# Moving one channel sum of the last image group from VectorE to ScalarE in a color-constancy kernel

## Chip, cores, metric

One core of a Trainium2 chip. The metric is device time in microseconds of one execution, median over runs. The sets of rounds ran on different chips, and the kernel before had a median of 22.99 to 23.03 us in each.

## The reference

```python
def reference(image):                      # float32 [16, 128, 128, 3]
    mean_rgb = np.mean(image, axis=(1, 2), keepdims=True)
    gray = np.mean(mean_rgb, axis=-1, keepdims=True)
    scale = gray / (mean_rgb + 1e-10)
    return np.clip(image * scale, 0, 1).astype(np.float32)
```

Every image has to be read wholly (three channel sums) before its first pixel can be scaled. The data is 3.15 MB in and 3.15 MB out, and it stays in SBUF, the core's own memory, in between. PSUM, named below, is the memory into which TensorE writes its results.

## The kernel before

Sixteen images are handled in four groups of four (g0 to g3). A group is one tile of 128 partitions x 512 pixels x 3 channels, 32 partitions per image.

```python
for g in range(G):                                     # G = 4
    nc.sync.dma_start(out=img_g, in_=src)              # L: load, 768 KB
    for c in range(2):                                 # A: ScalarE, sums of channels 0 and 1
        nc.scalar.activation(out=scr_p[:, 0:Q], in_=img_g[:, :, c], func=act.Copy,
                             accum_out=rows_g[:, c : c + 1])
    nc.vector.reduce_sum(out=rows_g[:, 2:3], in_=img_g[:, :, 2], axis=ax.X)   # R: VectorE, channel 2
    nc.tensor.matmul(psum_g, lhsT=blk, rhs=rows_g, start=True, stop=True)     # M: totals per image
    # D: denominator and total (from PSUM), C: reciprocal, S: scale   -- three tiny VectorE steps
    ... cut ...
    if g == G - 1:
        chunks = [(0, 320, nc.sync), (320, Q, nc.scalar)]   # last group: two stores
    else:
        chunks = [(0, Q, nc.sync)]
    for q0, q1, eng in chunks:
        for c in range(C):                             # O: VectorE, multiply and clip
            nc.vector.tensor_scalar(out=out_g[:, q0:q1, c], in0=img_g[:, q0:q1, c],
                scalar1=scale_g[:, c : c + 1], scalar2=1.0, op0=alu.mult, op1=alu.min)
        eng.dma_start(out=dst[:, q0 * C : q1 * C], in_=out_g[:, q0:q1, :])
```

The letters are used below: D3 is step D of group g3. The order on each engine is chosen by a scheduler. On VectorE it is R0 R1 D0 C0 S0 O0, D1 **R2** C1 S1 O1, D2 **R3** C2 S2 O2, D3 C3 S3 O3.

## Time and profile before

| | before |
|---|---|
| time, median of 16 runs in the rounds with the changed kernel | 23.0 us (22.92 to 23.1) |
| span of the profiled execution | 21.2 us |
| busy: VectorE / ScalarE / TensorE | 11.5 / 8.8 / 2.3 us |
| R: 4 reductions, mean | 825 ns |
| A: 8 ACTIVATEs, mean (plus accumulator read) | 853 ns (189 ns) |
| O: multiply pass over 512 pixels, mean | 560 ns |

Read it in stages: the loads keep DMA full to about 9.6 us (their last packets end at 10.5), then the stores follow as VectorE finishes each group, with pauses between them, and the last of them fill 4 us without a pause. VectorE is 54% busy over the span, but from 6.96 to 17.50 us it hardly rests (10.19 of 10.54 us busy). The lines are in the prediction.

### The profile page before, as it was taken

To read this page: it belongs to the slowest core of one execution; us is meant where nothing else is said; L and a number is where in the kernel's file an instruction comes from. 1 tells how busy PE (TensorE), PEld (TensorE's weight loads), DVE (VectorE), ACT (ScalarE), POOL (GpSimd) and SP (SyncE) were. 2 spreads that over 40 slices of the span, in tenths; PEclk is the share of its full clock that TensorE was granted. 3 is DMA by queue.
4 is the path that set the end of the run, shared out by engine and by line. 5 is a ranking of instruction groups with operands and counts; after the bars stand their busy time and mean duration, and the time that the engine had idled before them with its cause. 6 is when DMAs were issued, how large, how long until landed. Compare 5 with 4: busy or idle time off the path is not lost.

```text
span 21.2 us, 133 instructions
## 1 busy us (share of the span) xinstructions
PE 2.3 (11%) x8; PEld 2.0 (9%) x8; DVE 11.5 (54%) x40; ACT 8.8 (42%) x17; POOL 0.2 (1%) x4
## 2 busy tenths in 40 slices
PE   0000000000000550090046000540000000000000
PEld 0000000000000540090045000630000000000000
DVE  0360000003920898999989999899989990000000
ACT  0698000003999999999999991000000000000000
POOL 3000000000000000000000000000000000000000
DMA  0006999999999999983089980889708998999500
GB/s 0 0 0 151 325 395 406 418 418 395 418 395 430 406 430 441 406 360 128 23 360 383 395 348 0 372 372 453 290 0 372 430 430 335 436 399 376 196 0 0
DMA packets 1296, 6.29 MB, mean 297 GB/s; under 512 B 144, under 2 KB 144, under 8 KB 1296
## 3 DMA queue, kind: packets, MB, share of 16 engines
q1 hardware_dynamic: 1152, 6.00, 70.2%
q10 hardware_dynamic: 144, 0.29, 3.6%
HBM read 3.15 MB, written 3.15 MB: 297 GB/s over the span
## 4 chain that ended last, share of the span: by engine, by line
DVE 47%; DMA 27%; issue 2%; SPq 2%; DVEq 2%
DVE out_g L105 29%; DMA img_g<-in_image_dram 27%; DVE rows_g L69 11%; DVE scale_g L90 3%; DVE recip_g L88 3%; SPq L61 2%; DVE denom_g L78 2%; DVEq L139 2%
## 5 line engine op out<-in xcount | busy, mean ns | idle before, releaser
L63 ACT ACTIVATE scr_p<-img_g 128x512 f32<-128x512 f32 x8 | 6.8, 853 | 3.2 <-DMA img_g<-in_image_dram 3.1
L105 DVE TENSOR_SCALAR out_g<-img_g,scale_g 128x512 f32<-128x512 f32 (+2 forms) x15 | 6.4, 493 | 0.1
L69 DVE TENSOR_REDUCE rows_g<-img_g 128x1 f32<-128x512 f32 x4 | 3.3, 825 | 4.6 <-DMA img_g<-in_image_dram 4.6
L74 PE MATMUL psum_g<-rows_g,blk 128*128 128x3 f32 x8 | 2.3, 361 | 11.7 <-ACT scr_p L63 9.7
L74 PEld LDWEIGHTS psum_g<-rows_g,blk 128*128 128x128 f32 x8 | 2.0, 312 | 11.9 <-ACT scr_p L63 11.9
L63 ACT ACT_TABLE_LOAD x1 | 1.3, 1283 | 0.7 <-PEq L128 0.7
L63 ACT ACTIVATION_READ_ACCUMULATOR scr_p<-img_g 128x1 f32 x8 | 1.5, 189 | 0.0
L90 DVE SCALAR_TENSOR_TENSOR scale_g<-recip_g,tot_g 128x3 f32<-128x3 f32 x4 | 0.6, 161 | 0.1
L88 DVE RECIPROCAL recip_g<-denom_g 128x3 f32<-128x3 f32 x4 | 0.7, 167 | 0.1
L78 DVE TENSOR_SCALAR_CACHE_REDUCE denom_g<-psum_g 128x3 f32<-128x3 f32 x4 | 0.6, 156 | 0.0
L46 DVE MEMSET blk<- 128x128 f32 x1 | 0.2, 165 | 0.8 <-PEq L128 0.8
L48 DVE MEMSET blk<- 32x32 f32 x4 | 0.3, 85 | 0.2
L78 DVE DVE_READ_ACCUMULATOR denom_g<-psum_g 128x1 f32 x4 | 0.3, 84 | 0.0
L128 POOL MEMSET const-bfloat16-1.0<- 128x1 bf16 x1 | 0.1, 103 | 0.0
L128 POOL MEMSET const-float32-0.0<- 128x1 f32 x1 | 0.1, 100 | 0.2 <-issue 0.2
L128 POOL MEMSET const-uint8-127<- 128x1 uint8 x1 | 0.1, 102 | 0.0
L128 POOL MEMSET const-float32-1.0<- 128x1 f32 x1 | 0.1, 99 | 0.0
## 6 DMA issues: line engine op xcount, KB each, us to landing
img_g<-in_image_dram SPq DMA_DIRECT2D x4, 768.0 KB, 6.5
out_dram<-out_g SPq DMA_DIRECT2D x3, 768.0 KB, 3.3
out_dram<-out_g SPq DMA_DIRECT2D x1, 480.0 KB, 2.9
out_dram<-out_g ACTq DMA_DIRECT2D x1, 288.0 KB, 2.8
```

The source lines that it names most:

```text
L46: nc.vector.memset(blk, 0.0)
L48: nc.vector.memset(blk[j * PPB : (j + 1) * PPB, j * PPB : (j + 1) * PPB], 1.0)
L61: nc.sync.dma_start(out=img_g, in_=src)
L63: nc.scalar.activation(out=scr_p[:, 0:Q], in_=img_g[:, :, c], func=act.Copy, accum_out=rows_g[:, c : c + 1],)
L69: nc.vector.reduce_sum(out=rows_g[:, 2:3], in_=img_g[:, :, 2], axis=ax.X,)
L74: nc.tensor.matmul(psum_g, lhsT=blk, rhs=rows_g, start=True, stop=True)
L78: nc.vector.tensor_scalar(out=denom_g, in0=psum_g, scalar1=float(eps_sum), scalar2=None, op0=alu.add, op1=alu.add, accum_out=tot_g,)
L88: nc.vector.reciprocal(recip_g, denom_g)
L90: nc.vector.scalar_tensor_tensor(out=scale_g, in0=recip_g, scalar=1.0 / 3.0, in1=tot_g.broadcast_to([P, C]), op0=alu.mult, op1=alu.mult,)
L105: nc.vector.tensor_scalar(out=out_g[:, q0:q1, c], in0=img_g[:, q0:q1, c], scalar1=scale_g[:, c : c + 1], scalar2=1.0, op0=alu.mult, op1=al ...
L128: nc = _bacc.Bacc("TRN2", target_bir_lowering=False, num_devices=1)
L139: with _tile.TileContext(nc) as tc:
```

## The change

The intent is to shorten VectorE's work after the loads: the third sum of g3 goes to ScalarE, which is idle by then. The loop is also rewritten as a list of stages, traced in the order given, so that the scheduler no longer chooses.

```diff
+    ON_ACT = (3,)  # groups whose third sum ScalarE does too
+    PROGRAM = "L0 L1 L2 L3 A0 R0 M0 A1 R1 M1 D0 C0 S0 O0 D1 A2 R2 M2 C1 S1 O1 D2 A3 M3 C2 S2 O2 D3 C3 S3 O3".split()
...
-        for c in range(2):
-            nc.scalar.activation(
+            for c in range(3 if g in ON_ACT else 2):
+                pin(nc.scalar.activation(
                     out=scr_p[:, 0:Q], in_=..., func=act.Copy, accum_out=...[:, c : c + 1])
-        nc.vector.reduce_sum(out=rows_g[:, 2:3], in_=img_g[:, :, 2], axis=ax.X)
+        elif what == "R":  # VectorE: sum of channel 2
+            pin(nc.vector.reduce_sum(out=t["rows"][:, 2:3], in_=t["img"][:, :, 2], axis=ax.X))
...
+    for word in PROGRAM:
+        stage(word[0], int(word[1:]))
```

The list has no R3, and A3 has three sums. `pin` keeps an instruction in its place on its engine. Everything else builds to the same instructions in the same order, but for one added wait (O3's first pass also waits for load 3).

More of the change, by code (lines that the diff above doesn't have):

```diff
@@ L20 @@
     assert C == 3
-    G = 4
-    BPG = B // G
-    assert BPG * G == B
-    PPB = P // BPG
-    ROWS_PER_PART = (H * BPG) // P
-    Q = ROWS_PER_PART * W
+    sizes = [4, 4, 4, 4]
+    assert sum(sizes) == B
+    G = len(sizes)
     f32 = mybir.dt.float32
@@ L39 @@
     const = ctx.enter_context(tc.tile_pool(name="const", bufs=1))
-    io = ctx.enter_context(tc.tile_pool(name="io", bufs=G))
-    st = ctx.enter_context(tc.tile_pool(name="st", bufs=G))
-    ps = ctx.enter_context(tc.tile_pool(name="ps", bufs=G, space=bass.MemoryType.PSUM))
+    io = ctx.enter_context(tc.tile_pool(name="io", bufs=4))
+    st = ctx.enter_context(tc.tile_pool(name="st", bufs=4))
+    ps = ctx.enter_context(tc.tile_pool(name="ps", bufs=4, space=bass.MemoryType.PSUM))
     psd = ctx.enter_context(tc.tile_pool(name="psd", bufs=2, space=bass.MemoryType.PSUM))
-    blk = const.tile([P, P], f32, name="blk")
@@ L46 @@
-    nc.vector.memset(blk, 0.0)
-    for j in range(BPG):
-        nc.vector.memset(blk[j * PPB : (j + 1) * PPB, j * PPB : (j + 1) * PPB], 1.0)
-    for g in range(G):
-        rows = slice(g * (P * ROWS_PER_PART), (g + 1) * (P * ROWS_PER_PART))
-        src = img_rows[rows].rearrange("(p k) x -> p (k x)", k=ROWS_PER_PART)
-        dst = out_rows[rows].rearrange("(p k) x -> p (k x)", k=ROWS_PER_PART)
-        img_g = io.tile([P, Q, C], f32, name="img_g")
-        out_g = io.tile([P, Q, C], f32, name="out_g")
-        rows_g = st.tile([P, C], f32, name="rows_g")
-        psum_g = ps.tile([P, C], f32, name="psum_g")
-        scr_p = psd.tile([P, Q], f32, name="scr_p")
-        nc.sync.dma_start(out=img_g, in_=src)
-        for c in range(2):
-            nc.scalar.activation(
-                out=scr_p[:, 0:Q],
-                in_=img_g[:, :, c],
-                func=act.Copy,
-                accum_out=rows_g[:, c : c + 1],
-            )
-        nc.vector.reduce_sum(
-            out=rows_g[:, 2:3],
-            in_=img_g[:, :, 2],
-            axis=ax.X,
-        )
-        nc.tensor.matmul(psum_g, lhsT=blk, rhs=rows_g, start=True, stop=True)
-        denom_g = st.tile([P, C], f32, name="denom_g")
-        tot_g = st.tile([P, 1], f32, name="tot_g")
-        nc.vector.tensor_scalar(
-            out=denom_g,
-            in0=psum_g,
-            scalar1=float(eps_sum),
-            scalar2=None,
-            op0=alu.add,
-            op1=alu.add,
-            accum_out=tot_g,
-        )
-        recip_g = st.tile([P, C], f32, name="recip_g")
-        nc.vector.reciprocal(recip_g, denom_g)
-        scale_g = st.tile([P, C], f32, name="scale_g")
-        nc.vector.scalar_tensor_tensor(
-            out=scale_g,
-            in0=recip_g,
-            scalar=1.0 / 3.0,
-            in1=tot_g.broadcast_to([P, C]),
-            op0=alu.mult,
-            op1=alu.mult,
-        )
-        if g == G - 1:
-            chunks = [(0, 320, nc.sync), (320, Q, nc.scalar)]
-        else:
-            chunks = [(0, Q, nc.sync)]
-        for q0, q1, eng in chunks:
-            for c in range(C):
-                nc.vector.tensor_scalar(
-                    out=out_g[:, q0:q1, c],
-                    in0=img_g[:, q0:q1, c],
-                    scalar1=scale_g[:, c : c + 1],
-                    scalar2=1.0,
-                    op0=alu.mult,
-                    op1=alu.min,
-                )
-            eng.dma_start(out=dst[:, q0 * C : q1 * C], in_=out_g[:, q0:q1, :])
@@ new lines @@
+    blks = {}
+    for gb in sorted(set(sizes)):
+        ppb = P // gb
+        t = const.tile([P, P], f32, name=f"blk{gb}")
+        nc.vector.memset(t, 0.0)
+        for j in range(gb):
+            nc.vector.memset(t[j * ppb : (j + 1) * ppb, j * ppb : (j + 1) * ppb], 1.0)
+        blks[gb] = t
+    ON_ACT = (3,)
+    PROGRAM = "L0 L1 L2 L3 A0 R0 M0 A1 R1 M1 D0 C0 S0 O0 D1 A2 R2 M2 C1 S1 O1 D2 A3 M3 C2 S2 O2 D3 C3 S3 O3".split()
+    row0 = [sum(sizes[:g]) for g in range(G)]
+    S = [dict() for _ in range(G)]
@@ new lines, in stage @@
+    def stage(what, g):
+        t, GB = S[g], sizes[g]
+        rpp = (H * GB) // P
+        Q = rpp * W
+        rows = slice(row0[g] * H, (row0[g] + GB) * H)
+        pin = tc.keep_in_program_order
+        if what == "L":
+            src = img_rows[rows].rearrange("(p k) x -> p (k x)", k=rpp)
+            t["img"] = io.tile([P, Q, C], f32, name="img_g", tag=f"img{Q}")
+            pin(nc.sync.dma_start(out=t["img"], in_=src))
+        elif what == "A":
+            t["rows"] = st.tile([P, C], f32, name="rows_g")
+            scr_p = psd.tile([P, Q], f32, name="scr_p", tag=f"scr{Q}")
+            for c in range(3 if g in ON_ACT else 2):
+                pin(nc.scalar.activation(
+                    out=scr_p[:, 0:Q],
+                    in_=t["img"][:, :, c],
+                    func=act.Copy,
+                    accum_out=t["rows"][:, c : c + 1],
+                ))
+        elif what == "R":
+            pin(nc.vector.reduce_sum(
+                out=t["rows"][:, 2:3], in_=t["img"][:, :, 2], axis=ax.X
+            ))
+        elif what == "M":
+            t["psum"] = ps.tile([P, C], f32, name="psum_g")
+            nc.tensor.matmul(t["psum"], lhsT=blks[GB], rhs=t["rows"], start=True, stop=True)
+        elif what == "D":
+            t["denom"] = st.tile([P, C], f32, name="denom_g")
+            t["tot"] = st.tile([P, 1], f32, name="tot_g")
+            pin(nc.vector.tensor_scalar(
+                out=t["denom"],
+                in0=t["psum"],
+                scalar1=float(eps_sum),
+                scalar2=None,
+                op0=alu.add,
+                op1=alu.add,
+                accum_out=t["tot"],
+            ))
+        elif what == "C":
+            t["recip"] = st.tile([P, C], f32, name="recip_g")
+            pin(nc.vector.reciprocal(t["recip"], t["denom"]))
+        elif what == "S":
+            t["scale"] = st.tile([P, C], f32, name="scale_g")
+            pin(nc.vector.scalar_tensor_tensor(
+                out=t["scale"],
+                in0=t["recip"],
+                scalar=1.0 / 3.0,
+                in1=t["tot"].broadcast_to([P, C]),
+                op0=alu.mult,
+                op1=alu.mult,
+            ))
+        elif what == "O":
+            dst = out_rows[rows].rearrange("(p k) x -> p (k x)", k=rpp)
+            out_g = io.tile([P, Q, C], f32, name="out_g", tag=f"out{Q}")
+            if g == G - 1:
+                chunks = [(0, (Q * 5) // 8, nc.sync), ((Q * 5) // 8, Q, nc.scalar)]
+            else:
+                chunks = [(0, Q, nc.sync)]
+            for q0, q1, eng in chunks:
+                for c in range(C):
+                    pin(nc.vector.tensor_scalar(
+                        out=out_g[:, q0:q1, c],
+                        in0=t["img"][:, q0:q1, c],
+                        scalar1=t["scale"][:, c : c + 1],
+                        scalar2=1.0,
+                        op0=alu.mult,
+                        op1=alu.min,
+                    ))
+                pin(eng.dma_start(out=dst[:, q0 * C : q1 * C], in_=out_g[:, q0:q1, :]))
```

## The prediction

> **What bounds the kernel now.** The four image groups are called g0 to g3. For each: load (L), sums of channels 0 and 1 on ScalarE (A), sum of channel 2 on VectorE (R), a matmul that spreads totals (M), then on VectorE denominator (D), reciprocal (C), scale (S) and three multiply-and-clip passes (O), then a store. I read the page first (VectorE is busy 54% of the span, no engine is full on average), then the chain of work that ended last, in order of time, because a mean over load, middle and tail says nothing about the end:
>
> ```profile
> 6.96 0.83 DVE rows_g L69
> ...
> 12.49 0.07 DVE denom_g L78 x2
> 12.57 0.74 DVE rows_g L69
> 13.30 0.09 DVE recip_g L88
> 13.40 0.02 issue
> 13.42 0.17 DVE scale_g L90
> ```
>
> From 6.96 us, when g1's load lands, the chain stays on VectorE to 17.50 us. At 12.57 it holds a reduction that has nothing to do with g2, whose scale is being computed: it is R3, the sum for the next group, which the scheduler put between D2 and C2. The timeline, VectorE alone, shows the same with starts and lengths (first column start, second length, us):
>
> ```profile
> 12.40 0.16 DVE L78 TENSOR_SCALAR_CACHE_REDUCE denom_g<-psum_g 128x3 f32<-128x3 f32 x1
> 12.48 0.09 DVE L78 DVE_READ_ACCUMULATOR denom_g<-psum_g 128x1 f32 x1
> 12.48 0.82 DVE L69 TENSOR_REDUCE rows_g<-img_g 128x1 f32<-128x512 f32 x1
> 13.22 0.17 DVE L88 RECIPROCAL recip_g<-denom_g 128x3 f32<-128x3 f32 x1
> 13.42 0.16 DVE L90 SCALAR_TENSOR_TENSOR scale_g<-recip_g,tot_g 128x3 f32<-128x3 f32 x1
> 13.62 1.49 DVE L105 TENSOR_SCALAR out_g<-img_g,scale_g 128x512 f32<-128x512 f32 x3
> 15.02 0.15 DVE L78 TENSOR_SCALAR_CACHE_REDUCE denom_g<-psum_g 128x3 f32<-128x3 f32 x1
> 15.10 0.08 DVE L78 DVE_READ_ACCUMULATOR denom_g<-psum_g 128x1 f32 x1
> 15.21 0.17 DVE L88 RECIPROCAL recip_g<-denom_g 128x3 f32<-128x3 f32 x1
> ```
>
> Here D2 to C2 (12.40 to 13.22) takes 0.82 us; D3 to C3 (15.02 to 15.21), with no reduction between, takes 0.19. ScalarE and TensorE for g3, in the same timeline:
>
> ```profile
> 10.80 0.87 ACT L63 ACTIVATE scr_p<-img_g 128x512 f32<-128x512 f32 x1
> 11.58 0.19 ACT L63 ACTIVATION_READ_ACCUMULATOR scr_p<-img_g 128x1 f32 x1
> 11.80 0.86 ACT L63 ACTIVATE scr_p<-img_g 128x512 f32<-128x512 f32 x1
> 12.60 0.19 ACT L63 ACTIVATION_READ_ACCUMULATOR scr_p<-img_g 128x1 f32 x1
> 13.42 0.50 PEld L74 LDWEIGHTS psum_g<-rows_g,blk 128*128 128x128 f32 x2 [2.04 <-ACT scr_p L63]
> 13.45 0.56 PE L74 MATMUL psum_g<-rows_g,blk 128*128 128x3 f32 x2 [1.98 <-DVE recip_g L88]
> ```
>
> ScalarE is done at 12.79 and stays idle until it issues the last store. M3 waited for R3, not for ScalarE. The last view is the busy time in stretches; columns are stretch, length, busy us of PE, PEld, DVE, ACT, POOL, then clock, DMA share, GB/s:
>
> ```profile
> 12.60:13.30 0.70, 0.00 (x0) 0.00 (x0) 0.70 (x2) 0.19 (x2) 0.00 (x0) 1.00 0.01 0
> 13.30:15.30 2.00, 0.56 (x2) 0.50 (x2) 1.90 (x9) 0.00 (x0) 0.00 (x0) 1.00 0.96 393
> 15.30:15.85 0.55, 0.00 (x0) 0.00 (x0) 0.48 (x3) 0.00 (x0) 0.00 (x0) 1.00 0.01 0
> 15.85:17.50 1.65, 0.00 (x0) 0.00 (x0) 1.65 (x6) 0.00 (x0) 0.00 (x0) 1.00 0.99 406
> 17.50:19.90 2.40, 0.00 (x0) 0.00 (x0) 0.00 (x1) 0.00 (x0) 0.00 (x0) 1.00 0.94 376
> ```
>
> DMA stands still for 0.70 us before g1's store and 0.55 us before g2's, because VectorE hasn't finished the data; from 15.85 on it is full to the end of the data (19.90). So the end is set by when g2's store starts, and that by VectorE.
>
> **What the Trainium skill says.** "ScalarE: Activation LUTs", section "What ACT_TABLE_LOAD costs", gives 186 ns + 0.833 N for an ACTIVATE with immediate scale and bias: 613 ns for 512 elements. The trace disagrees: mean 853 ns (strided input, accumulator) plus a 189 ns accumulator read; I use the trace. "VectorE: DVE Perf Modes", section "The perf-mode tier table", has tensor_reduce at 1x always and fp32 tensor_scalar at 2x. The trace has the same order: 825 ns for the reduction, 560 for a multiply pass of the same 512 elements. So the reduction is the dear VectorE instruction, and ScalarE does the same work in nearly the same time. "Perfetto Trace Analysis", section "Identifying Dependency Chains", says that an instruction that waits on several engines may have an EventSemaphore put before it. The build of the changed kernel shows one: O3's first pass now waits for load 3 as well as for its scale. "DMA: Bandwidth & Descriptors", section "Issuing engines are not separate DMA queues", says that SP's and ACT's transfers share 16 engines; the trace agrees, the last two stores (480 KB and 288 KB, 768 together) run at a share of 0.94.
>
> **The change part by part.** Most of the diff only rewrites the loop as an explicit list of stages. The instruction order of both builds, engine by engine, differs in three places only; the memsets, loads, stores, chunks, pools in use and the order D1, R2, C1 are the same.
> 1. VectorE loses R3 (1 of 4 reductions, 825 ns).
> 2. ScalarE gets a third ACTIVATE for g3 (853 + 189 ns), after the two it has.
> 3. M3 waits for ScalarE alone; O3's first pass gets the extra wait on load 3.
>
> VectorE's new times: D2 stays at 12.40. C2 follows 0.19 later as D3 to C3 does: 12.59 instead of 13.22, 0.62 to 0.63 earlier (not 0.825, since the reduction overlaps its neighbours and C2 would have waited 0.19 for D2's result anyway). S2 12.80, O2 from 13.00; D3 could start 1.40 after O2's start (13.62 to 15.02 before): 14.40 instead of 15.02.
>
> When is g3's psum ready? Within a group ScalarE starts the second ACTIVATE 0.99 to 1.02 after the first (10.80 to 11.80). The third then starts at 12.80, its accumulator read starts 0.80 later and ends at 13.79. M starts 0.05 after the accumulator read has ended (g2: 10.83 to 10.88), so M3 is at 13.84 instead of 13.42, that is 0.42 later. D0 started at 7.75 with M0 at 7.12: 0.63. D3 is therefore at 13.84 + 0.63 = 14.47. The later of 14.40 and 14.47 counts: VectorE waits about 0.07 and D3 moves from 15.02 to 14.47, 0.55 earlier. C3, S3 and O3 keep their lengths, O3 ends at 16.95 instead of 17.50.
>
> The extra wait costs nothing by my reckoning: load 3 landed by 10.80, when A3 starts, and O3 must anyway wait for S3 (0.16 us), behind which a passed wait is hidden.
>
> Stores: g2's is issued 0.62 earlier, and its data starts at 15.85 - 0.62 = 15.23, just where g1's ends (15.30), so about 0.07 of that is lost to the queue. The two last stores are issued 0.55 earlier. From there the tail is as it was: about 4.05 us of full DMA, then 1.3 us for landing and the end. Both ways of reckoning give 0.55. 23.0 - 0.55 = 22.45 us, 2.4% less.
>
> **The rivals.**
> - R1, the wait is replaced: the third ACTIVATE is on a new critical path, L3 to three ACTIVATEs to M3 to D3. I reckon that it costs 0.07. For more: A3 starts right when load 3 lands, so a load 0.1 later, which the old VectorE chain hid, would now move the end. If that path is 0.2 later than I reckon, only 0.35 is left: 22.65 us, within 2%. Against: spacing and matmul latency repeat to a few hundredths in all groups.
> - R2, the DMA takes the gain: from g1's store on, 2.36 MB now go out nearly without a pause. If the queue doesn't keep its 0.94 to 0.99 share, 0.1 to 0.3 of the gain is lost: 22.55 to 22.75. Against: g2's and g3's stores already run back to back now for 4 us at this rate.
> - R3, all of it arrives: load 3 lands earlier in ordinary executions, or the matmul is quicker, and D3 follows at 14.40: gain 0.62, 22.38 us. If the whole 825 ns counted, 22.18; the overlap in the trace speaks against it.
> - R4, slower: the added wait stalls VectorE's queue, or ScalarE is slowed beside VectorE. Nothing in the trace shows either; A1 and A2 ran beside VectorE with the same 0.84 to 0.87 us.
>
> **Range and chances.** My number is the sum's 22.45. The line for "faster by over 2%" is 22.54, a gain of 0.46, which leaves a margin of 0.09. R1 and R2 are the likely ways to lose that margin, R3 pulls the other way; the executions before spread over 0.12 us. I give a range of 22.33 to 22.62, and 0.73 for faster, 0.26 for the same, 0.01 for slower.
>
> **What would show it right or wrong.** In the profile after: 9 ACTIVATEs, 3 reductions; D2 to C2 0.19 to 0.20; M3 at 13.8 to 13.9, released by ScalarE; D3 about 14.47 with a VectorE gap of under 0.1 before it, put down to TensorE; O3's end near 16.95; the 0.55 pause of the DMA before g2's store gone, the 0.70 pause before g1's store still there; span near 20.6. A gap before D3 of 0.2 or more means R1; D3 on time with O3 ending on time but the data ending later than 19.4 means R2; a gap between S3 and O3 beyond the former 0.2 start to start means R4. I am wrong altogether if g2's scale isn't earlier by about 0.6, since then the reduction wasn't what C2 waited for.

## The result, and the profile after

| | before | after |
|---|---|---|
| time, median | 23.0 us (16 runs) | 22.44 us (11 runs, 22.38 to 22.58) |
| ratio, 95% interval | | 0.9763 (0.9741 to 0.9785): faster |
| span of the profiled execution | 21.2 us | 20.6 us |
| busy: VectorE / ScalarE | 11.5 / 8.8 us | 10.9 / 9.8 us |

A ratio is the mean time of one kernel's fast runs over the mean of the other's of the same rounds, so it isn't quite the ratio of the medians. Executions over 1.5% slower than the fastest of the same kernel are left out of the means.

The timeline after, VectorE (start, length, us):

```profile
12.44 0.14 DVE L87 TENSOR_SCALAR_CACHE_REDUCE denom_g<-psum_g 128x3 f32<-128x3 f32 x1
...
12.63 0.18 DVE L98 RECIPROCAL recip_g<-denom_g 128x3 f32<-128x3 f32 x1
12.84 0.16 DVE L101 SCALAR_TENSOR_TENSOR scale_g<-recip_g,tot_g 128x3 f32<-128x3 f32 x1
13.03 1.50 DVE L118 TENSOR_SCALAR out_g<-img_g,scale_g 128x512 f32<-128x512 f32 x3
14.46 0.16 DVE L87 TENSOR_SCALAR_CACHE_REDUCE denom_g<-psum_g 128x3 f32<-128x3 f32 x1
...
15.07 1.88 DVE L118 TENSOR_SCALAR out_g<-img_g,scale_g 128x320 f32<-128x320 f32 x6
```

D2 to C2 is 0.19 us now, O2 starts at 13.03 instead of 13.62, D3 at 14.46 instead of 15.02, O3 at 15.07 instead of 15.62. The same timeline, ScalarE's third sum and M3:

```profile
12.80 0.86 ACT L71 ACTIVATE scr_p<-img_g 128x512 f32<-128x512 f32 x1
13.58 0.20 ACT L71 ACTIVATION_READ_ACCUMULATOR scr_p<-img_g 128x1 f32 x1
...
13.83 0.50 PEld L83 LDWEIGHTS psum_g<-rows_g,blk 128*128 128x128 f32 x2 [2.45 <-ACT scr_p L71]
```

M3 comes 0.41 us later than before and is released by ScalarE. The busy time in stretches (stretch, length, PE, PEld, DVE, ACT, POOL, clock, DMA share, GB/s):

```profile
12.60:13.30 0.70, 0.00 (x0) 0.00 (x0) 0.60 (x3) 0.67 (x3) 0.00 (x0) 1.00 0.01 0
13.30:15.25 1.95, 0.58 (x2) 0.50 (x2) 1.84 (x8) 0.48 (x2) 0.00 (x0) 1.00 0.99 403
15.25:15.35 0.10, 0.00 (x0) 0.00 (x0) 0.10 (x1) 0.00 (x0) 0.00 (x0) 1.00 0.03 0
15.35:16.90 1.55, 0.00 (x0) 0.00 (x0) 1.55 (x6) 0.00 (x0) 0.00 (x0) 1.00 1.01 412
16.90:19.40 2.50, 0.00 (x0) 0.00 (x0) 0.05 (x1) 0.00 (x0) 0.00 (x0) 1.00 0.94 374
```

This view counts a packet wholly in the stretch in which it starts, so a share can come out above 1, and the end of a store can look like a pause while its last packets still run. By the packets themselves the pause ahead of g2's store is gone: before, g1's last packet ended at 15.42 and g2's first began at 15.97, 0.55 us later; after, they are at 15.48 and 15.42. The pause ahead of g1's store, 0.70 us in this view and 0.56 by packets (0.59 after), is still there, as nothing ahead of it changed. The time that came off the end, 0.56 us, is about the pause that went.

### The profile page after: what moved, and what is told of

Read it like the earlier page. It is cut to its first block, busy times and chain, and to the rows that moved or that the text cites.

```text
span 20.6 us, 134 instructions
## 1 busy us (share of the span) xinstructions
PE 2.4 (11%) x8; PEld 2.0 (10%) x8; DVE 10.9 (53%) x39; ACT 9.8 (48%) x19; POOL 0.2 (1%) x4
## 4 chain that ended last, share of the span: by engine, by line
DVE 46%; DMA 28%; issue 2%; SPq 2%; DVEq 2%
DVE out_g L118 29%; DMA img_g<-in_image_dram 28%; DVE rows_g L78 8%; DVE scale_g L101 3%; DVE recip_g L98 3%; DVE denom_g L87 2%; SPq L66 2%; DVEq L155 2%
## 5 line engine op out<-in xcount | busy, mean ns | idle before, releaser
L71 ACT ACTIVATE scr_p<-img_g 128x512 f32<-128x512 f32 x9 | 7.7, 850 | 3.3 <-DMA img_g<-in_image_dram 3.1
L78 DVE TENSOR_REDUCE rows_g<-img_g 128x1 f32<-128x512 f32 x3 | 2.5, 835 | 4.6 <-DMA img_g<-in_image_dram 4.6
```

The costliest lines, as they stand in the source:

```text
L71: pin(nc.scalar.activation(out=scr_p[:, 0:Q], in_=t["img"][:, :, c], func=act.Copy, accum_out=t["rows"][:, c : c + 1],))
L78: pin(nc.vector.reduce_sum(out=t["rows"][:, 2:3], in_=t["img"][:, :, 2], axis=ax.X))
```

## The experiments

Two theories about what sets the end:

- **Theory A**: the end follows VectorE's own end, that is D3 and O3. Then ScalarE's new path to D3 is critical, and every delay of D3 is a delay of the end.
- **Theory B**: the end follows the moment when g2's store starts, since from there DMA has 4 us of stores to move. Then D3 and O3 have slack.

Both predict the 0.55 us, so the changed kernel alone can't tell them apart. All edits below are against the changed kernel. This table sums up what was measured. The three columns of packets count from the first load packet of the same trace (1.73 to 1.79 us into the span), so that they can be compared between runs. They belong to one profiled execution, the time to the median of all. The runs that are not in it, e10, e8 and e9, are told below.

| run | time, median | ratio to before (95%) | D3 starts | g2's store, first packet | g3's store, first packet | last packet |
|---|---|---|---|---|---|---|
| before | 23.0 | 1 | 15.02 | 14.23 | 16.15 | 18.25 |
| changed | 22.44 | 0.976 (0.974 to 0.979) | 14.46 | 13.68 | 15.60 | 17.69 |
| e1_undo | 23.02 | 0.999 (0.997 to 1.002) | 15.06 | 14.28 | 16.20 | 18.30 |
| e3_no_sum3 | 22.43 | 0.977 (0.972 to 0.983) | 14.44 | 13.67 | 15.59 | 17.70 |
| e4_act_small | 22.44 | 0.975 (0.971 to 0.980) | 14.57 | 13.62 | 15.55 | 17.67 |
| e4_act_big | 22.80 | 0.990 (0.987 to 0.994) | 15.13 | 13.63 | 15.92 | 18.04 |
| e11_g2_store_late2 | 22.99 | 0.999 (0.998 to 1.001) | 14.58 | 14.18 | 16.10 | 18.18 |
| e2_r3_in_o2 | 23.24 | 1.011 (1.008 to 1.014) | 15.62 | 14.48 | 16.50 | 18.60 |
| e5_g2_g3_act | 23.14 | 1.005 (1.003 to 1.007) | 15.41 | 13.80 | 16.25 | 18.37 |
| e12_no_r2 | 22.28 | 0.967 (0.964 to 0.970) | 14.79 | 13.15 | 15.64 | 17.76 |

### e1_undo: the rewrite without the move

```diff
-    ON_ACT = (3,)
+    ON_ACT = ()
-    ... D2 A3 M3 C2 S2 O2 ...
+    ... D2 A3 R3 M3 C2 S2 O2 ...
```

> The changed kernel's explicit list of stages, but R3 back on VectorE between D2 and C2 and two ACTIVATEs for g3, so that VectorE has the instruction order of the kernel before. If the gain comes from moving R3 (my theory): 23.0 us, ratio to before 0.998 to 1.002, D2 to C2 0.82 us again. If the rewrite as a list of stages is worth something by itself: below 22.9.

23.02 us, ratio 0.9994. The whole gain belongs to the move of R3, and the list of stages is worth nothing by itself. The timeline of e1_undo has the reduction back between D2 and C2, with D2 (12.46) to C2 at 0.82 us:

```profile
12.54 0.81 DVE L78 TENSOR_REDUCE rows_g<-img_g 128x1 f32<-128x512 f32 x1
13.28 0.15 DVE L98 RECIPROCAL recip_g<-denom_g 128x3 f32<-128x3 f32 x1
```

### e3_no_sum3: the third sum done by nobody (wrong)

```diff
-    ON_ACT = (3,)
+    ON_ACT = ()
+    rows3 = const.tile([P, C], f32, name="rows3");  nc.vector.memset(rows3, 256.0)   # g3's sums start from this
```

> Wrong result on purpose: g3's third sum is not done by any engine, a constant stands in its place. M3 is then ready at about 12.85, long before VectorE wants D3. Theory A (the end follows D3 and O3 on VectorE, as the prediction has it): D3 at 14.40 instead of 14.46, 22.38 us, 0.06 below the changed kernel. Theory B (the end follows the moment when g2's store starts, after which DMA runs full for 4 us; O3 has slack): 22.44, no difference. The difference is small and may not be resolved; what it shows for certain is whether ScalarE's third sum costs more than 0.1 us.

22.43 us, the same as the changed kernel within the run to run spread. ScalarE's third sum, 0.85 + 0.19 us of work, is free as far as this resolves (the interval of the ratio is 0.12 us to either side). M3 started at 13.10, and D3 at 14.44 instead of 14.46. The constant is close to the true sums of this random input, so the output even passed the comparison, as that of e12_no_r2 below did; that says nothing for them as kernels.

### e4_act_small and e4_act_big: a later D3

```diff
             for c in range(3 if g in ON_ACT else 2):
+                if g == 3 and c == 2:
+                    extra = st.tile([P, N], f32, name="extra")       # N = 4 or 512
+                    pin(nc.scalar.activation(out=extra, in_=t["img"][:, 0:N, 2], func=act.Copy))
```

> The changed kernel plus one tiny ACTIVATE (128x4, into a tile of its own) between the second and the third sum of g3; estimated from the spacing of the ACTIVATEs in the trace, it delays M3 and D3 by 0.2 to 0.3 us and leaves g2's store alone. Theory A: the end moves with D3, 22.65 to 22.75 us. Theory B: 22.44, since the first store of g3 is issued at 16.5 instead of 16.2, its data could start at 17.2, and DMA is busy with g2's store until 17.35 anyway.

> As e4_act_small, with an extra ACTIVATE of 128x512: D3 later by 0.8 to 0.9 us, to about 15.3. Theory A: 22.44 + 0.85 = 23.3 us. Theory B: the first store of g3 is issued at about 17.05, its data starts at about 17.75 instead of 17.35, so only about 0.4 of the 0.85 reaches the end: 22.85 us.

The small one failed as an edit: the tiny ACTIVATE (at 12.78) fits into a gap, and the third sum starts 1.02 us after the second (11.90 and 12.92), as in the changed kernel (11.78 and 12.80). D3 was 0.11 us later all the same (14.57), because load 3's last packet ended 0.10 later in this execution (10.58 instead of 10.47) and A3 began 0.10 later (10.88 instead of 10.78). So by chance its trace shows what a later load does: D3 moved, and the end did not (22.38 us in this execution, 22.44 in the median). The big one had D3 0.67 us later, at 15.13, less than the 0.8 to 0.9 expected, since it too fills the gap: it starts 0.87 after the second sum and the third sum 0.78 after it, 1.65 in place of 1.02. The time rose by 0.36 us. So 0.3 us of the delay vanished. The timeline and the stretches of e4_act_big:

```profile
15.13 0.16 DVE L90 TENSOR_SCALAR_CACHE_REDUCE denom_g<-psum_g 128x3 f32<-128x3 f32 x1 [0.59 <-PE psum_g L86]
...
15.35:15.85 0.50, 0.00 (x0) 0.00 (x0) 0.43 (x3) 0.00 (x0) 0.00 (x0) 1.00 0.96 393
...
17.35:17.65 0.30, 0.00 (x0) 0.00 (x0) 0.27 (x2) 0.00 (x0) 0.00 (x0) 1.00 0.02 0
17.65:19.40 1.75, 0.00 (x0) 0.00 (x0) 0.00 (x0) 0.00 (x0) 0.00 (x0) 1.00 0.96 381
```

and the changed kernel in the same stretch:

```profile
17.35:17.65 0.30, 0.00 (x0) 0.00 (x0) 0.00 (x0) 0.00 (x0) 0.00 (x0) 1.00 1.08 435
```

In the changed kernel DMA goes from g2's store to g3's without a pause, because g3's first store has been waiting behind it. In e4_act_big it runs dry: the 0.3 us of waiting are used up, and the rest is a pause. This is the slack of D3: 0.67 - 0.36 = 0.31 us by the times. It can be read off the changed kernel itself, from the issue of the two stores:

```profile
14.56 0.33 SPq L126 DMA_DIRECT2D out_dram<-out_g  x1
...
16.21 0.33 SPq L126 DMA_DIRECT2D out_dram<-out_g  x1
```

g3's first store is issued 1.65 us after g2's, but its first packet follows g2's by 1.92 (15.60 - 13.68), so it stands in the queue for 0.27. Say 0.3. Theory A is refuted.

### e10_g2_store_late and e11_g2_store_late2: D3 on time, g2's store late

```diff
+                if g == 2:
+                    part = out_g[:, 0:256, 2]        # e10: channel 0
+                    pin(nc.scalar.activation(out=part, in_=part, func=act.Copy))
                 pin(eng.dma_start(out=dst[:, q0 * C : q1 * C], in_=out_g[:, q0:q1, :]))
```

> The changed kernel, but an in-place copy on ScalarE (128x256 of g2's output) stands between O2 and g2's store, so that store is issued 0.6 to 0.75 us later while D3, O3 and the stores of g3 are issued as before. The opposite of e4: there D3 was late and g2's store on time. Theory A (VectorE's end sets the end): 22.44 us. Theory B (the start of g2's store sets it): 22.44 + 0.7 = 23.05 to 23.2 us, with DMA pausing 0.7 us before g2's store and then full to the end.

This one failed as an experiment: the copy of channel 0 depended on the first pass of O2 alone and ran at 13.80, ahead of the last pass. The store was issued 1.60 us after O2's start, against 1.53 in the changed kernel. The 22.58 us (4 runs) tell nothing about A and B. In its profiled execution the first load landed 0.2 us later than usual and everything after it was late by about as much; why, is open.

> e10 mended: its copy touched channel 0 only, which the first pass of O2 had already written, so it ran early and delayed the store by 0.07 us at most. Here the in-place copy (128x256) touches channel 2, which the last pass of O2 writes, so g2's store is issued about 0.65 to 0.7 us later (15.2 to 15.25), with D3, O3 and the issue of g3's stores unchanged. Theory A (end follows VectorE's D3 and O3): 22.44 us. Theory B (end follows the start of g2's store): 23.05 to 23.15 us.

The mended copy waited for the last pass:

```profile
14.52 0.54 ACT L128 ACTIVATE out_g<-out_g 128x256 f32<-128x256 f32 x1 [0.61 <-DVE out_g L118]
...
15.08 0.33 SPq L129 DMA_DIRECT2D out_dram<-out_g  x1
...
15.35:15.85 0.50, 0.00 (x0) 0.00 (x0) 0.50 (x2) 0.00 (x0) 0.00 (x0) 1.00 0.00 0
...
19.40:19.90 0.50, 0.00 (x0) 0.00 (x0) 0.00 (x0) 0.00 (x0) 0.00 (x0) 1.00 0.83 323
```

g2's store was issued at 15.08 instead of 14.56, 0.52 later (0.65 to 0.7 was expected, since the copy took less time than I took it to), and the time is 22.99: the whole gain is gone, though VectorE still does no R3. D3 was at 14.58, where e4_act_small's 14.57 cost nothing. 0.52 us of delay at the store gave 0.55 us at the end. Theory B holds.

### e12_no_r2: what more could be had (wrong)

```diff
+    rows2 = const.tile([P, C], f32, name="rows2");  nc.vector.memset(rows2, 256.0)   # g2's sums start from this
-    ... A2 R2 M2 ...
+    ... A2 M2 ...
```

> Wrong result on purpose: the changed kernel without g2's third sum, a constant in its place, to see what taking R2 off VectorE could give if it cost nothing elsewhere. g1's and g2's stores start about 0.65 earlier, D3 stays at 14.46 because ScalarE's path holds it. Theory A: 22.44 us, nothing gained. Theory B: g2's data ends at about 16.7, g3's first store (issued at 16.21) starts at about 16.9 instead of 17.35, so 22.0 us.

22.28 us: less than Theory A's 22.44, more than the 22.0 I expected from Theory B. With g2's store 0.54 us earlier, D3's slack is used up and D3's path takes over: the timeline of e12_no_r2 shows VectorE waiting for it.

```profile
14.79 0.16 DVE L92 TENSOR_SCALAR_CACHE_REDUCE denom_g<-psum_g 128x3 f32<-128x3 f32 x1 [0.79 <-PE psum_g L88]
```

It is 2.1 us from g3's first packet to the last in every run of the table, so only g3's start matters, and its store can come no more than the slack of 0.3 us earlier as long as D3 stays at 14.46. I had put this at 0.45; with 0.3 the time would be 22.15. The rest up to 22.28 isn't settled. The profiled execution was the slowest of the six (22.46 us) and its load 3 landed late (g3's first ACTIVATE at 11.11 instead of 10.78), which now, with no slack left, goes straight to the end. So a further gain on VectorE ends after 0.3 us at most (0.16 was measured), unless ScalarE's path is shortened too.

### e5_g2_g3_act: the same move once more

```diff
-    ON_ACT = (3,)                ... A2 R2 M2 ...
+    ON_ACT = (2, 3)              ... A2 M2 ...
```

> The same move for g2 too: VectorE loses R2 as well, ScalarE does three sums for g2 and for g3. g1's store starts 0.65 us earlier, but ScalarE becomes the bound: D2 about 12.5 (no earlier than now) and D3 about 15.35 instead of 14.46. Theory A: 22.44 + 0.9 = 23.3 us. Theory B, with e4_act_big's slack of 0.3 in D3: 22.44 + 0.6 = 23.0 us. If moving reductions off VectorE is good without limit: 21.8 to 22.0 us.

23.14 us, so the gain is lost and a little more. VectorE waited 0.63 us for D2 (12.55) and 0.73 us for D3 (15.41), both times for the matmul behind ScalarE. D3's 0.95 us of delay, less the slack of 0.3, gives 0.65; 0.70 was measured.

### e2_r3_in_o2: the reduction where it hides nothing

```diff
-    ... D2 A3 M3 C2 S2 O2 D3 ...
+    ... D2 A3 C2 S2 O2 M3 D3 ...          # ON_ACT = ()
                 for c in range(C):
+                    if g == 2 and c == 2:
+                        stage("R", 3)
```

> R3 back on VectorE, not between D2 and C2 but between the second and the third pass of O2, where no wait of a dependent instruction hides part of it. If my reckoning of the hidden part is right (0.62 of 0.825 us counted between D2 and C2, because C2 would have waited 0.19 anyway), it costs 0.72 to 0.77 us here: g2's store at 15.3, D3 about 15.5. Theory B: 23.15 to 23.2 us, 0.15 above e1_undo and the kernel before. Theory A (D3 1.04 later than in the changed kernel): 23.45 us. If the place makes no difference: 23.0 us.

23.24 us, 0.25 above the kernel before of the same rounds (22.99). The reduction and the pass after it in the timeline:

```profile
14.06 0.82 DVE L78 TENSOR_REDUCE rows_g<-img_g 128x1 f32<-128x512 f32 x1
14.79 0.56 DVE L120 TENSOR_SCALAR out_g<-img_g,scale_g 128x512 f32<-128x512 f32 x1
15.62 0.16 DVE L87 TENSOR_SCALAR_CACHE_REDUCE denom_g<-psum_g 128x3 f32<-128x3 f32 x1 [0.27 <-PE psum_g L83]
```

Start to start the reduction takes 0.73 us (14.06 to 14.79), and between D2 and C2 it had cost 0.82 - 0.19 = 0.63. So the hidden part is real, some 0.1 us of it by a wait that was there anyway, the rest by overlap with its neighbours. The time rose by more than the expected 0.15 to 0.2 because M3 now came so late (VectorE waited 0.27 us for it) that D3's path, not g2's store, set the end.

### e8_pool_half and e9_pool_tree: GpSimd as a helper

```diff
+            if g == 2:                                   # e8; e9 goes on to 128 and 64 and puts R2 into O1
+                h = st.tile([P, Q // 2], f32, name="half")
+                pin(nc.gpsimd.tensor_tensor(out=h, in0=t["img"][:, 0 : Q // 2, 2],
+                                            in1=t["img"][:, Q // 2 : Q, 2], op=alu.add))
+                pin(nc.vector.reduce_sum(out=t["rows"][:, 2:3], in_=h, axis=ax.X))
```

> The changed kernel, with GpSimd adding the two halves of g2's channel 2 (128x256) as soon as load 2 is in, so that R2 on VectorE has 256 elements instead of 512 and D1 to C1 is about 0.28 us shorter. ScalarE's path to D3 stays at 14.46. Theory A: D3 is held by ScalarE, 22.44 us. Theory B: both g1's and g2's store start 0.28 earlier, 22.15 to 22.2 us. If GpSimd's addition is slow beside VectorE's multiply passes and ends after 9.9, R2 waits for it and the gain is gone or turns into a loss.

> As e8, with three additions on GpSimd (256, 128, 64), and R2 over the 64 that are left moved between the first and second pass of O1, where nothing should wait for it. Theory B: g1's store about 0.4 earlier, D2 about 12.0, g2's store about 0.4 earlier; g3's first store is then bound by ScalarE's path (issue at 16.21), so 22.05 to 22.15 us. Theory A: 22.44. If GpSimd ends after 10.9, VectorE waits inside O1 and the gain is lost.

22.80 us (ratio to before 0.990) and 22.73 us (0.987): both slower than the changed kernel. R2 did get shorter: D1 to C1 fell to 0.41 us. But in e8_pool_half O0 took 2.25 us instead of 1.50:

```profile
8.99 1.35 POOL L80 TENSOR_TENSOR half<-img_g 128x256 f32<-128x256 f32 x1 [8.55 <-DMA img_g<-in_image_dram]
...
9.40 1.31 DVE L121 TENSOR_SCALAR out_g<-img_g,scale_g 128x512 f32<-128x512 f32 x1
```

One multiply pass took 1.31 us instead of 0.56, and ended at 10.71, only after GpSimd's addition had (10.34). I had expected GpSimd to be the one that is held up. The Trainium skill has it, "SBUF — State Buffer", section "Who interferes with whom": VectorE's 2-port modes, which tensor_scalar can use, and GpSimd share a port pair, and whoever comes first holds it for its whole instruction. That fits this trace, though no run here tests it apart. It is a loss of 0.75 us on VectorE for a gain of 0.41.

## Why the prediction was right, point by point

- **R3 stood between D2 and C2 and cost 0.62 us there.** Right. D2 to C2 went from 0.82 to 0.19 us, and O2 started 0.59 earlier (13.62 to 13.03; D2 itself was 0.04 later in this execution). e1_undo brought all of it back, and e2_r3_in_o2 bears out that it wasn't the full 825 ns.
- **ScalarE's third sum and M3.** Right to 0.01 us: M3 at 13.83 (13.84 predicted), D3 at 14.46 (14.47). The added wait on load 3 showed nothing: S3 to O3 is 0.20 us, as before.
- **DMA is full from g2's store to the end, so the start of that store sets the end.** Right, and shown by e11_g2_store_late2. The sizes: the issue of g2's store moved by 0.58 us (15.14 to 14.56; 0.62 predicted), of which 0.03 were lost to the queue behind g1's store (0.07 predicted), so that its first packet moved by 0.55, as predicted: the two differences of 0.04 cancel. The prediction took the start of the data from the edge of a stretch, 15.85; the first packet came at 15.97, and as both kernels shift alike, the sum stands.
- **"The later of 14.40 and 14.47 counts", and the rival R1: a load 0.1 later "would now move the end".** This step was wrong as a statement about the end. D3 has 0.3 us of slack behind g2's store, so ScalarE's path cost nothing (e3_no_sum3, where D3 could start at 14.44, so the wait was 0.02 us and not 0.07), nor did a load 0.10 later (e4_act_small's trace). The two reckonings gave 0.55 both, and I took the agreement for support; but only the second one, through g2's store, was the reason, and that the first gave the same number was luck. The slack could have been had from the profile before: g3's first store was issued 1.62 us after g2's (16.76 and 15.14), and its first packet came 1.92 after g2's.
- **The rival R2, DMA takes the gain.** It didn't: DMA held shares of 0.94 to 1.01 from 13.30 to 19.40, but for the 0.1 us ahead of g2's store in which no packet of data starts.
- **The rivals R3 and R4.** Neither happened. Even with D3 earlier, the rival R3 would have given nothing, as e3_no_sum3 shows.

No version that was tried and is correct beats the changed kernel. What is left open is the 0.2 us by which loads were late in some executions (e10's above all).

## What to carry to other kernels

When a tail is a chain of stores, look for the first store after which DMA never pauses again: what releases that store is worth its full length, and what feeds a later store has slack until the queue in front of it is empty. Moving work to an idle engine is free up to that slack and no further, so the second such move (e5) lost all that the first had won. Where two ways of reckoning agree on a number, find out which of them is the cause, by delaying each alone.

## What the Trainium skill lacked or had wrong

- "ScalarE: Activation LUTs", "What ACT_TABLE_LOAD costs": its formula for immediate operands, from which I estimate 613 ns for 512 elements, doesn't fit the ACTIVATEs here, which read every third fp32 element: 850 ns mean in the changed kernel, and 191 ns more for the accumulator read. Within a group they start 0.98 to 1.02 us apart. The summing is not what makes them long: the extra ACTIVATE of e4_act_big reads the same input, doesn't sum, and takes 872 ns. With the 538 ns of e11's copy of 256 elements and the 209 ns of e4_act_small's 4 elements I estimate about 0.2 us + 1.3 ns for each element, so it is the part for each element that is larger than the page's. No run here reads contiguous elements, so that the stride is the reason is not shown.
- "DMA: Bandwidth & Descriptors", "Latency and other measured facts", gives about 600 ns to the first byte. Here a store that found DMA idle took 0.83 us from the start of its issue to its first packet: issued at 15.08 with the first packet at 15.91 in e11_g2_store_late2, 15.14 and 15.97 in the kernel before. From which moment the page counts it doesn't say.
- No page that I read tells how to find the slack of a store behind a busy queue; here it was 0.3 us, and it decided what the extra ScalarE work cost (nothing).
